# Stores of the scan's columns issued from GpSimd's queue instead of SyncE's, in a one-core RWKV-7 and neighbourhood-attention trunk

## Chip, cores and metric

The kernel runs on one core of a Trainium2 chip. The metric is the device time of one execution in microseconds, as a median of several executions. A core has five engines, each of which works through its own queue of instructions in order: TensorE (PE, with its weight loads PEld), VectorE (DVE), ScalarE (ACT), GpSimd (POOL) and SyncE (SP). In this kernel SP does nothing but issue DMA transfers. An instruction waits at the head of its engine's queue until the semaphores that it names are reached, and what stands behind it on that engine waits too.

## What is computed

Two independent requests (x_prompt and x_sample, 512 tokens of 1024 features each) go through two layers with shared weights. Layer 0 is a bidirectional RWKV-7 branch, layer 1 a gated neighbourhood attention. Cut to what matters:

```python
for i in range(2):                                   # layers
    xn = rms_norm(x, pre_norm_g[i])
    h = rwkv7(xn) if i == 0 else natten(xn)
    x = x + rms_norm(h, post_norm_g[i])

# rwkv7: r, k, v from token-shifted xn, z from xn (four 1024x1024 projections)
for d in range(2):                                   # forward and backward scan, 16 heads of 64
    S_t = S_(t-1) (diag(decay_t) + a_t b_t^T) + v_t k_t^T ;  y_t = S_t r_t
y = group_norm(y[0] + y[1]) + sum_d sum(r * k_d * r_k) * v
out = (y * silu(z)) @ w_o
# natten: q, k, v, z = split(xn @ w_in + b_in); windowed softmax attention; (o * silu(z)) @ w_ao + b_ao
```

## The kernel before

**Layout and tiles.** Activations lie with features on the 128 partitions and the 512 tokens of a request along the free axis, so that a tensor of a request is eight tiles of 128x512 f32 (256 KB). A request is called s = 0 or 1, and the eight tiles are p = 0 to 7 (a tile holds two heads). A projection is done a column at a time: one column is one output tile, 8 contraction tiles by 3 matmuls (lines 802 to 804 in the scan; weights and activations are each split in two parts, `whi` and `wlo`, `act` high and low). The weights of a column come in two loads `raw` of 128x512 through three buffers (NRAW), are split by ACT (line 721) and DVE (line 723), and wait in four buffers (NW).

**Stages.** A prelude normalises both requests, makes the z and k columns of request 0 and stores the shifted operands (`lk`, `lr`, `lv`, `lz`) of request 1 to DRAM. Then `scan_phase` (about 190 to 1180 us) does the scan: eight blocks (two requests by four pairs of tiles) of eight steps, 64 steps one after the other. Beside the steps, in the same phase, run: `flow` (the remaining columns, r and v of request 0, k, r, v and z of request 1, w_o of request 0, and 24 columns of layer 1), `prep` (per tile: decay, keys, the array `ab` that goes to DRAM as `dab`), `inverse` (DVE's elimination per block) and `finish` (per block: normalisation and gate, `dy`). Last, `rest` does the remaining projections, the attention and the output.

**What goes through DRAM.** `save(kind, s, p, src)` at line 323 makes a DRAM tile and stores `src` into it, from SP (line 325). Column results are written by ACT or DVE into `tmp` tiles (five buffers, NTMP) and saved as `dr`, `dk`, `dv`, `dz` and, for layer 1, `q1`, `k1`, `v1`, `z1` (named `dq`, `dk`, `dv`, `dz` in the profile). `prep` saves the head sums' products `ks` (line 968, `dks<-kp`). The v column is also transposed by TensorE (line 680), copied by ACT into `vs` (line 683, two buffers, NVS) and stored by token as `dvt`: four stores of 64x512 a column at lines 685 to 687, each of 512 runs of 256 bytes. The scan loads V (line 1047) and X (lines 1055 to 1057) from `dvt`, `prep` loads k and r, `finish` loads ks, v and z. All of these loads and stores stand in one queue, SP's.

**What POOL does.** In the scan phase only memsets: the border column of `e1` in `prep` (line 893, 32 of them) and half of `MT` in `inverse` (line 1014, 16).

**What sets the order.** PE, DVE and ACT follow in the scan phase an order written by a planner (`weave`, line 1600): threads for the parts above are taken by rank as soon as a model of the machine (`Clock`) says that their inputs are there. The model gives a DMA from SP 380 ns of its queue (line 131), a share of one common transfer queue (`dq`) and a landing time. Where the model sees PE without work it puts in a matmul whose result is not used (line 1626), to keep PE's clock up. The orders of SP's and POOL's queues are made by the scheduler of the tile framework, by the times at which it expects each instruction to be ready. A waiting instruction therefore holds up the ones that were placed behind it.

Of the kernel before, what the change touches and what calls it, by code (L numbers as in the profile page):

```python
# [19 lines left out]
P = 128  # L20
# [30 lines left out]
class Clock:  # L51
# [40 lines left out]
    def room(self, key, bufs):  # L92
        s = self.slots.get(key, ())
        return 0.0 if len(s) < bufs else min(self.left(n) for n in s)
# [18 lines left out]
    def one(self, e, i):  # L113
        ap = lambda xs: [x for x in xs if hasattr(x, "bass_ap")]
        outs, ins = ap(i.outs), ap(i.ins)
        if not outs:
            return 0.0
        name = lambda x: x.bass_ap.tensor.name
        t = issued = self.t[e]
        for table, xs in ((self.made, ins), (self.used, outs)):  # L120
            for x in xs:
                for f, at in table.get(name(x), {}).items():
                    if f != e or e == "S" or e in "AD" and table is self.made:
                        t = max(t, at)
        free = lambda x: int(np.prod([n for _, n in x.ap[1:]])) if len(x.ap) > 1 else 1
        n = max([free(outs[0])] + [free(x) for x in ins[:1]])
        if e == "P":
            t, done = self.matmul(i, ins, free(outs[0]), t)
        elif e == "S":

            self.t[e] = issued = max(issued, self.t["P"]) + 380.0
            size = outs[0].ap[0][1] * free(outs[0]) * 4
            c = size * 0.0027 + 150.0
            self.dq = max(issued + 800.0, self.dq) + c
            done = max(self.dq, t + 800.0 + c) + 670.0
        else:
            if e == "A":
                c = 85.0 + 0.85 * n
            elif e == "G":
                c = 150.0 + n  # L140
            else:
                kind = type(i).__name__
                sb = [x for x in ins if free(x) > 8 and not name(x).startswith(self.BANKS)]
                c = 82.0 + 1.02 * n
                if "Reciprocal" in kind:
                    c = 80.0 + 6.2 * n
                elif getattr(i, "is_tensor_tensor_scan", False):
                    c = 80.0 + 2.1 * n
                elif "Transpose" in kind:
                    c = 80.0 + 1.8 * n  # L150
                elif len(sb) == 1 and len(ins) <= 2 and "TensorTensor" not in kind and "Reduce" not in kind and free(outs[0]) == n:
                    c = 110.0 + 0.53 * n if not getattr(i, "is_scalar_tensor_tensor", False) else 130.0 + 1.06 * n
            self.t[e] = t + c
            done = t + c + self.LAT[e]
        for x in ins:
            u = self.used.setdefault(name(x), {})
            u[e] = max(u.get(e, 0.0), done)
            self.slot[name(x)] = True
        for x in outs:
            for table in (self.used, self.made):  # L160
                u = table.setdefault(name(x), {})
                u[e] = max(u.get(e, 0.0), done)
        return 0.0 if e == "S" and "dram" in str(type(outs[0].bass_ap.tensor)).lower() else done

    def matmul(self, i, ins, n, t):
        f32, tr = ins[0].dtype == F32, bool(i.is_transpose)
# [63 lines left out]
class Trunk:  # L230
# [17 lines left out]
    SUMS, SG, ZY = 0, 0, 2  # L248
# [22 lines left out]
    def name(self, s):  # L271
        self.uid += 1
        return f"{s}_{self.uid}"
# [29 lines left out]
    def t(self, tag, shape=(P, T), bufs=1, dt=F32, pool=None):  # L303
        x = (pool or self.main).tile(list(shape), dt, tag=tag, bufs=bufs, name=self.name(tag))
        self.clock.new(x.tensor.name, (tag, id(pool or self.main)), bufs)
        return x
# [15 lines left out]

    def save(self, kind, s, p, src):
        self.sp[kind, s, p] = d = self.dram(f"{kind}{s}{p}", src.shape)
        self.nc.sync.dma_start(d, src)

    def load(self, dst, src):
        self.nc.sync.dma_start(dst, src)
# [111 lines left out]
    def rstd(self, acc):  # L440
        run(self.rstds(acc))
        return acc
# [165 lines left out]
    def column(self, s, kind, p, ps):  # L608

        nc, sp = self.nc, self.sp  # L610
        vt, act = nc.vector, nc.scalar
        first = lambda e: (e, None, lambda c, n=ps.tensor.name: c.at([n]))
        keep, whole = self.clock.keep, ps.tensor.name
        if kind == "z":

            o, th = self.tmp(), self.tmp()
            if s == 0:
                yield first("D")
                vt.tensor_tensor(o, ps, self.rstd0, op=ALU.mult)
                ps = o  # L620
            yield "A" if s == 0 else first("A")
            keep.add(whole)
            act.activation(th, ps, AF.Tanh, scale=0.5)
            yield "D"
            keep.discard(whole)
            vt.scalar_tensor_tensor(o, th, 1.0, ps, op0=ALU.add, op1=ALU.mult)
            self.save("z", s, p, o)
            return
        yield "A", None, lambda c: max(c.at([ps.tensor.name]), min(c.room(("tmp", id(self.main)), self.NTMP), 1e10))
        o = self.tmp()  # L630
        if kind == "k":
            keep.add(whole)
        act.copy(o, ps)
        self.save(kind, s, p, o)
        if kind == "r":
            self.made.add((kind, s, p))
            return
        if kind == "k":
            yield "A"
            keep.discard(whole)  # L640
            sq = self.tmp()
            act.activation(sq, ps, AF.Square, scale=self.vec("kk", p))
            free, room = self.bank()
            yield "P", free, lambda c: max(room(c), c.at([sq.tensor.name]))
            ss = self.p("pm", (2, T))
            nc.tensor.matmul(ss, self.ssel, sq, start=True, stop=True)
            yield "A"
            row = self.tmp((2, T))
            act.copy(row, ss)
            if p == 0:  # L650
                sp["ss", s] = self.dram(f"ss{s}", (16, T))
            self.load(sp["ss", s][2 * p:2 * p + 2], row)
            self.made.add((kind, s, p))
            if p == NP - 1:
                yield "S", None, lambda c: c.at([sp["ss", s].tensor.name])

                rn = self.tmp((P, 64))
                self.load(rn, sp["ss", s].rearrange("a (b c) -> (a b) c", b=8))
                yield "A"
                act.activation(rn, rn, AF.Sqrt)  # L660
                yield "D"
                vt.tensor_scalar(rn, rn, 1e-12, None, op0=ALU.max)
                vt.reciprocal(rn, rn)
                sp["rn", s, 0] = self.dram(f"rn{s}", (16, T))
                self.load(sp["rn", s, 0].rearrange("a (b c) -> (a b) c", b=8), rn)
                self.made.add(("rn", s))
            return

        if p == 0:

            sp["vt", s] = self.dram(f"vt{s}", (4, 2, NCH // 2, 2, L, 2, 2, HD))
        yield "A"
        back = self.tmp()
        act.copy(back, o[:, ::-1])
        for d in range(2):
            free, room = self.bank()
            yield "P", free, lambda c: max(room(c), c.at([back.tensor.name]))
            vp = self.p("pm")
            for m in range(4):
                nc.tensor.transpose(vp[:, m * P:(m + 1) * P], (back if d else o)[:, m * P:(m + 1) * P], self.ident)  # L680
            yield "A", None, lambda c: max(c.at([vp.tensor.name]), c.room(("vs", id(self.main)), self.NVS))
            vs = self.t("vs", (P, 4, P), self.NVS)
            act.copy(vs, vp.rearrange("p (m c) -> p m c", m=4))
            for j in range(2):
                self.load(
                    sp["vt", s][p // 2, j, :, :, :, d, p % 2].rearrange("m h t c -> t (m h) c"),
                    vs[64 * j:64 * j + 64].rearrange("t m (h c) -> t (m h) c", h=2))
        self.made.add((kind, s, p))
# [952 lines left out]
    def scan_phase(self, mid):  # L1641
        t = lambda tag, shape: self.t(tag, shape, 1, F32, self.front)
        did = self.did
        self.mrx = t("mrx", (P, 2, 2, L))
        for d in range(2):
            self.nc.vector.tensor_copy(self.mrx[:, d], self.mr[d].unsqueeze(1).broadcast_to([P, 2, L]))
# [64 lines left out]
        e = mybir.EngineType  # L1711
# [4 lines left out]
    def run(self):  # L1716
# [2 lines left out]
        self.did = Counter()  # L1719
        self.xz, self.os = [], [[], []]  # L1720
        self.spare = None
        mid, prep, first = ExitStack(), ExitStack(), ExitStack()
        self.banks(mid, pf=1, pm=5 - self.SG - self.ZY, us=1)
        if self.SG:
# [18 lines left out]
        self.rest(prep, mid)  # L1743

    def rest(self, prep, mid):
        prep.close()
        mid.close()
        self.banks(self.stack, pg=self.PG, pt=self.PT, po=1, sc=1, pm=5 - self.PG - self.PT)
# [166 lines left out]
```

## Time and profile before

| | us |
|---|---|
| median of 3 runs | 1694.72 (1691.98 to 1698.94) |
| profiled execution, its own time | 1691.19 |
| span of the profiled execution | 1689.4 |
| prelude, 0 to 190: PE busy | 169.51 of 190 |
| scan phase, 190 to 1180: PE busy | 913.97 of 990 |
| rest, 1180 to 1690: PE busy | 488.80 of 510 |
| POOL busy in the whole span | 24.2 |
| mean granted TensorE clock | 0.971 |

The profile lists each engine's instructions with their times. Idle time in front of an instruction is put down to what released it. "SPq" rows are SP's DMA issues: their length is the time that SP's queue spent on issuing, not the transfer. A transfer's landing is seen only where an instruction waited for it. PE's records overlap, so a busy PE is not necessarily at its peak, and the matmuls of line 1626 count as busy although nothing uses them.

### The profile page before, as it was taken

To read this page: it belongs to the slowest core of one execution; us is meant where nothing else is said; L and a number is where in the kernel's file an instruction comes from. 1 tells how busy PE (TensorE), PEld (TensorE's weight loads), DVE (VectorE), ACT (ScalarE), POOL (GpSimd) and SP (SyncE) were. 2 spreads that over 40 slices of the span, in tenths; PEclk is the share of its full clock that TensorE was granted. 3 is DMA by queue.
4 is the path that set the end of the run, shared out by engine and by line. 5 is a ranking of instruction groups with operands and counts; after the bars stand their busy time and mean duration, and the time that the engine had idled before them with its cause. 6 is when DMAs were issued, how large, how long until landed. Compare 5 with 4: busy or idle time off the path is not lost. (4 is left out here: it accounts for less than half of the span.)

```text
span 1689.4 us, 46296 instructions
## 1 busy us (share of the span) xinstructions
PE 1572.3 (93%) x18820; PEld 1201.0 (71%) x18820; DVE 1229.1 (73%) x2725; ACT 982.1 (58%) x1977; POOL 24.2 (1%) x94
## 2 busy tenths in 40 slices
PE   7989888899988998989988999999999898999998
PEld 5767666676766766767766767777787687777776
DVE  8985668689678787887888888745676766465564
ACT  5443655677765768656566665444676655555562
POOL 0000000000000000000000000000000000000000
PEclk9989999899999999999998999999999899999999
DMA  5435678688587787775776765554765246545553
GB/s 208 162 125 187 202 231 260 181 253 267 183 262 229 215 263 238 229 245 181 231 254 209 220 206 165 171 186 138 269 205 172 86 124 240 189 149 176 167 176 106
DMA packets 240821, 336.26 MB, mean 199 GB/s; under 512 B 53696, under 2 KB 119360, under 8 KB 240608
## 3 DMA queue, kind: packets, MB, share of 16 engines
q1 hardware_dynamic: 240608, 333.31, 61.9%
q8 instruction: 148, 2.42, 0.6%
q14 instruction: 65, 0.53, 0.1%
HBM read 227.71 MB, written 105.51 MB: 197 GB/s over the span
## 5 line engine op out<-in xcount | busy, mean ns | idle before, releaser
L802 PE MATMUL pm<-act,whi 128*128 128x512 f32 x640 | 284.9, 445 | 17.2 <-ACT act L747 4.3
L804 PE MATMUL pm<-act,wlo 128*128 128x512 f32 x640 | 258.0, 403 | 10.0 <-DVE wlo L723 9.9
L803 PE MATMUL pm<-act,whi 128*128 128x512 f32 x640 | 258.4, 404 | 7.4 <-DVE act L749 6.4
L423 PE MATMUL pg<-act,whi 128*128 128x512 f32 x448 | 184.0, 412 | 3.1 <-ACT os L1494 1.9
L424 PE MATMUL pg<-act,whi 128*128 128x512 f32 x448 | 179.2, 400 | 4.8 <-DVE act L373 4.8
L425 PE MATMUL pg<-act,wlo 128*128 128x512 f32 x448 | 179.0, 399 | 0.0
L372 ACT CAST whi<-raw 128x512 fp32r<-128x512 f32 x148 | 91.3, 618 | 131.1 <-PE pg L424 87.2
L802 PEld LDWEIGHTS pm<-act,whi 128*128 128x128 f32 x640 | 122.8, 192 | 62.2 <-issue 11.5
L804 PEld LDWEIGHTS pm<-act,wlo 128*128 128x128 f32 x640 | 123.4, 193 | 42.2 <-DVE wlo L723 15.1
L803 PEld LDWEIGHTS pm<-act,whi 128*128 128x128 f32 x640 | 123.5, 193 | 33.3 <-DVE act L749 12.4
L373 DVE TENSOR_TENSOR wlo<-raw,whi 128x512 fp32r<-128x512 f32 x148 | 101.7, 689 | 61.7 <-ACT whi L372 56.2
L723 DVE TENSOR_TENSOR wlo<-raw,whi 128x512 fp32r<-128x512 f32 x160 | 109.1, 685 | 36.5 <-ACT whi L721 33.2
L721 ACT CAST whi<-raw 128x512 fp32r<-128x512 f32 x160 | 98.4, 617 | 58.1 <-PE pm L803 27.5
L424 PEld LDWEIGHTS pg<-act,whi 128*128 128x128 f32 x448 | 85.6, 191 | 22.0 <-DVE act L373 5.2
L423 PEld LDWEIGHTS pg<-act,whi 128*128 128x128 f32 x448 | 85.3, 191 | 21.9 <-issue 3.0
L425 PEld LDWEIGHTS pg<-act,wlo 128*128 128x128 f32 x448 | 85.5, 191 | 18.1 <-issue 0.7
L996 DVE TENSOR_TENSOR N<-etmp,N 128x30 f32<-128x30 f32 (+14 forms) x240 | 78.8, 328 | 4.2
L994 DVE TENSOR_TENSOR etmp<-N 128x30 f32<-128x30 f32 (+14 forms) x240 | 78.6, 328 | 4.1
L1448 DVE CUSTOM_DVE_ANT_0 sb<-sc,bias 128x256 f32<-128x256 f32 x128 | 49.9, 420 | 40.3 <-PE pt L1455 26.4
L1451 ACT ACTIVATE sb<-sb,mx 128x256 f32<-128x256 f32 x128 | 64.1, 503 | 11.0 <-DVE mx L1450 10.8
L1090 PE MATMUL pf<-cab 64*64 64x128 f32 (+1 forms) x2048 | 66.3, 265 | 1.9 <-issue 1.9
L1201 ACT COPY X<-us 64x256 f32<-64x256 f32 x128 | 47.0, 367 | 33.3 <-PE zy L1068 30.1
(389 smaller groups left out, 3370.9 us busy)
## 6 DMA issues: line engine op xcount, KB each, us to landing
dab<-ab SPq DMA_DIRECT2D x32, 1024.0 KB
cab<-dab SPq DMA_DIRECT2D x64, 512.0 KB
raw<-in_w_in_dram SPq DMA_DIRECT2D x128, 256.0 KB
bias<-in_rpb_dram SPq DMA_DIRECT2D x32, 384.0 KB
raw<-in_w_z_dram SPq DMA_DIRECT2D x32, 256.0 KB
dz<-tmp SPq DMA_DIRECT2D x32, 256.0 KB
raw<-in_w_k_dram SPq DMA_DIRECT2D x32, 256.0 KB
dk<-tmp SPq DMA_DIRECT2D x32, 256.0 KB
```

Of the source, the lines that this page charges most:

```text
L372: self.nc.scalar.copy(hi, src)
L373: (eng or self.nc.vector).tensor_tensor(lo, src, hi.bitcast(F32), op=ALU.subtract)
L423: nc.tensor.matmul(ps, hi, x[k][0], start=(k == 0), stop=False)
L424: nc.tensor.matmul(ps, hi, x[k][1], start=False, stop=False)
L425: nc.tensor.matmul(ps, lo, x[k][0], start=False, stop=(k == KT - 1))
L721: nc.scalar.copy(hi, raw[h])
L723: nc.vector.tensor_tensor(lo, raw.pop(h), hi.bitcast(F32), op=ALU.subtract)
L802: nc.tensor.matmul(ps, hi[:, at], xh, start=(k == 0), stop=False)
L803: nc.tensor.matmul(ps, hi[:, at], xl, start=False, stop=False)
L804: nc.tensor.matmul(ps, lo[:, at], xh, start=False, stop=(k == KT - 1))
L994: vt.tensor_tensor(tv, N[:, q + 1:, q:q + 1].broadcast_to([P, n, q]), N[:, q:q + 1, :q].broadcast_to([P, n, q]), op=ALU.mult)
L996: vt.tensor_tensor(N[:, q + 1:, :q], tv, N[:, q + 1:, :q], op=ALU.add)
```

## The change

While `scan_phase` runs (`self.away` is True there and False before and after), `save` issues its stores from POOL's queue for every kind except y, x1 and h, and so do the stores of v by token. These are 152 DMAs: 16 of r, 16 of v, 8 of k and 8 of z of layer 0, 16 of `ks`, 64 of `dvt`, and 6 each of q, k, v and z of layer 1. The small stores of k's sums of squares (`dss`), the stores of `ab`, y, x1 and h, and all loads stay on SP.

The planner's model is told of it: a DMA from POOL takes 900 ns of POOL's queue in the model, where one from SP takes 380, and its waits and landing are reckoned as an SP store's. Since the planner's times change, the whole order of PE, DVE and ACT in the scan phase is planned anew.

```diff
@@ Clock.one
-                    if f != e or e == "S" or e in "AD" and table is self.made:
+                    if f != e or e in "SG" or e in "AD" and table is self.made:
...
-        elif e == "S":
-
-            self.t[e] = issued = max(issued, self.t["P"]) + 380.0
+        elif e == "S" or type(i).__name__ == "InstDMACopy":
+            if e == "G":
+                self.t[e] = issued = max(issued, self.t["P"]) + 900.0
+            else:
+                self.t[e] = issued = max(issued, self.t["P"]) + 380.0
...
-        return 0.0 if e == "S" and "dram" in str(type(outs[0].bass_ap.tensor)).lower() else done
+        return 0.0 if e in "SG" and "dram" in str(type(outs[0].bass_ap.tensor)).lower() else done
@@ Trunk
     def save(self, kind, s, p, src):
         self.sp[kind, s, p] = d = self.dram(f"{kind}{s}{p}", src.shape)
-        self.nc.sync.dma_start(d, src)
+        self.store(kind).dma_start(d, src)
+
+    def store(self, kind):
+        return self.nc.gpsimd if self.away and kind not in ("y", "x1", "h") else self.nc.sync
@@ column
             for j in range(2):
-                self.load(
+                self.store("vt").dma_start(
                     sp["vt", s][p // 2, j, :, :, :, d, p % 2].rearrange("m h t c -> t (m h) c"),
@@ scan_phase
+        self.away = True
@@ run, rest
+        self.away = False
```

The instructions below are listed as they stand in each engine's queue, with the buffer numbers; line numbers of the changed kernel are 2 to 8 higher from line 130 on (line 802 is 807 there, 1626 is 1631).

POOL's queue in the scan's first part, before (`e1` is the array of decays of a prep, `MT0` the inverse's buffer of a block):

```order
L893 MEMSET e1_580_2300 128x8
L893 MEMSET e1_647_2551 128x8
L893 MEMSET e1_674_2686 128x8
L893 MEMSET e1_748_3091 128x8
L1014 MEMSET MT0_439_1696 32x32x32 x2
L893 MEMSET e1_779_3317 128x8
```

The same stretch of POOL's queue now (`tmp` is a column's result, `kp0` the product that is stored as `dks`, `vs` a transposed v tile):

```order
L898 MEMSET e1_666_2609 128x8
L327 DMA dks01_620_2457<-kp0_575_2246 128x512
L327 DMA dv00_645_2521<-tmp_644_2519 128x512
L327 DMA dv01_655_2575<-tmp_654_2573 128x512
L690 DMA dvt0_646_2523<-vs_670_2620 64x8x64 x2
L898 MEMSET e1_690_2752 128x8
L690 DMA dvt0_646_2523<-vs_672_2630 64x8x64 x2
L690 DMA dvt0_646_2523<-vs_684_2685 64x8x64 x2
L327 DMA dv02_695_2764<-tmp_694_2762 128x512
L898 MEMSET e1_765_3192 128x8
```

Between two memsets of `e1` there now stand up to eighteen stores, and a store can stand behind a memset: `dks01` and `dv00` come after the memset of e1_666.

SP's queue before, where the first v columns of request 0 are stored and the first step's V and X are loaded:

```order
L328 DMA raw_691_2790<-in_w_v_dram 128x512
L328 DMA dvt0_659_2585<-vs_695_2814 64x8x64 x2
L325 DMA dv02_700_2829<-tmp_699_2827 128x512
L325 DMA dks02_701_2832<-kp0_662_2597 128x512
L328 DMA dvt0_659_2585<-vs_702_2834 64x8x64 x2
L328 DMA X_705_2844<-dvt0_659_2585 64x2x128
L328 DMA raw_707_2851<-in_w_v_dram 128x512
L328 DMA tmp_713_2865<-in_lora2_dram 128x512
L328 DMA r_709_2858<-dr03_521_2015 128x512
L328 DMA raw_732_2988<-in_w_v_dram 128x512
L328 DMA dvt0_659_2585<-vs_718_2896 64x8x64
L328 DMA V_703_2838<-dvt0_659_2585 128x256
```

The same place of SP's queue now:

```order
L333 DMA dab01_632_2489<-ab_668_2615 128x8x256
L333 DMA raw_700_2783<-in_w_v_dram 128x512
L333 DMA rb_733_2997<-drn0_411_1636 64x512 x2
L333 DMA X_699_2780<-dvt0_646_2523 64x2x128
L333 DMA X_727_2950<-dvt0_646_2523 64x2x128
L333 DMA raw_721_2933<-in_w_v_dram 128x512
L333 DMA k_731_2995<-dk03_302_1318 128x512
L333 DMA dab01_632_2489<-ab_692_2758 128x8x256
L333 DMA V_697_2774<-dvt0_646_2523 128x256
L333 DMA X_699_2780<-dvt0_646_2523 64x2x128
L333 DMA V_698_2777<-dvt0_646_2523 128x256
```

The stores `dvt`, `dv` and `dks` are gone from between the loads, and the loads of V and X wait here for stores that another queue issues.

PE's queue after the first r column, before (line 1626 is the matmul without use, 872 and 873 the decays of the first prep, 802 to 804 a product of the next column):

```order
L1626 MATMUL zy_444_1710<-cc_143 128x256 x2
L872 MATMUL pm_480_1835<-h0_126_633,w2h_472_1793 128x512
L873 MATMUL pm_480_1835<-h0_126_633,w2l_471_1792 128x512
L1626 MATMUL zy_444_1710<-cc_143 128x256
L872 MATMUL pm_486_1848<-h2_137_669,w2h_472_1793 128x512
L873 MATMUL pm_486_1848<-h2_137_669,w2l_471_1792 128x512
L1626 MATMUL zy_444_1710<-cc_143 128x256
L802 MATMUL pm_487_1853<-act_414_1641,whi_482_1840 128x512
L803 MATMUL pm_487_1853<-act_413_1640,whi_482_1840 128x512
```

And now:

```order
L1631 MATMUL zy_444_1710<-cc_143 128x256 x3
L877 MATMUL pm_480_1836<-h0_126_633,w2h_472_1793 128x512
L878 MATMUL pm_480_1836<-h0_126_633,w2l_471_1792 128x512
L1631 MATMUL zy_444_1710<-cc_143 128x256
L877 MATMUL pm_486_1849<-h2_137_669,w2h_472_1793 128x512
L878 MATMUL pm_486_1849<-h2_137_669,w2l_471_1792 128x512
L807 MATMUL pm_487_1853<-act_414_1641,whi_482_1841 128x512
L808 MATMUL pm_487_1853<-act_413_1640,whi_482_1841 128x512
```

From here on the two orders differ everywhere. Over the whole program PE's queue holds 98 matmuls of line 1626 before and 105 now; 108 products (threes of lines 802 to 804) stand ahead of the first scan step's outputs (line 1213) before and 129 now, with 44 and 35 matmuls of line 1626; behind the first output of the last step there are 27 products before and 16 now, and none and 3 matmuls of line 1626.

More of the change, by code (lines that the diff above doesn't have):

```diff
@@ L1745, in rest @@
     def rest(self, prep, mid):
+        self.away = False
         prep.close()
```

## The prediction

> **What bounds the kernel now.** I read the head of the page first, then the busy time of each stage, then who waits for whom in the scan phase on PE, ACT and SP, then the rows of the stores that move. The change acts between 190 and 1180 us alone; a row of stages shows what room is there.
>
> ```profile
> span 1689.4 us, 46296 instructions
> PE 1572.3 (93%) x18820; PEld 1201.0 (71%) x18820; DVE 1229.1 (73%) x2725; ACT 982.1 (58%) x1977; POOL 24.2 (1%) x94
> ...
> 190.00:1180.00 990.00, 913.97 (x15391) 688.52 (x15391) 767.75 (x1481) 609.22 (x1184) 18.70 (x47) 0.97 0.69 217
> ...
> L1626 PE MATMUL zy<-cc 128*128 128x256 f32 x196 | 50.0, 391 | 0.5 <-ACT Z L1174 0.5
> ```
>
> In the scan phase PE is busy 914 of 990 us, so 76 us are idle; 47 to 50 us of the busy time are the matmuls that nothing uses. PE's other work does not change. So the phase can become shorter by part of some 125 us at most, and it becomes longer by whatever stalls PE anew. DVE, with 768 of 990, is the second engine. Next, what PE's idle time was waiting for:
>
> ```profile
> PE pm L804 <- DVE wlo L723: 9.9, 9, 3.5
> PE pm L803 <- DVE act L749: 6.4, 11, 2.4
> ...
> PE pm L802 <- ACT act L747: 4.3, 5, 1.9
> ...
> PE zy L1068 <- DMA cab<-dab: 2.7, 2, 1.5
> ```
>
> ```profile
> ACT whi L721 <- DMA raw<-in_w_r_dram: 9.6, 3, 4.8
> ACT whi L721 <- DMA raw<-in_w_v_dram: 9.5, 4, 4.7
> ```
>
> PE waited directly for a load for 2.7 us only. Late weights reach it through ACT's and DVE's splits (lines 721, 723, 747 and 749); these waits are 9.9 + 6.4 + 4.3 us, and ACT waited for r's and v's weights 9.6 and 9.5 us. So 9.9 + 6.4 + 4.3 + 2.7 = 23.3 us is all of PE's idle time in these rows that earlier loads could remove, if each of them were a load's fault.
>
> **What leaves SP.** The rows of the issues (least, median and longest in ns) price it, and a piece of SP's order in time shows the place where it is densest:
>
> ```profile
> L325 SPq DMA_DIRECT2D dz<-tmp x32: 319/326/732, 44.5 to 1645.2; - x32
> L325 SPq DMA_DIRECT2D dk<-tmp x32: 319/359/1548, 99.5 to 1611.7; - x32
> L325 SPq DMA_DIRECT2D dv<-tmp x32: 319/422/1493, 266.0 to 1620.3; - x32
> ...
> L325 SPq DMA_DIRECT2D dr<-tmp x16: 319/330/1638, 185.4 to 551.2; - x16
> L325 SPq DMA_DIRECT2D dks<-kp x16: 319/392/622, 214.0 to 1000.3; - x16
> ...
> L325 SPq DMA_DIRECT2D dq<-tmp x16: 319/377/435, 942.1 to 1603.4; - x16
> ...
> L328 SPq DMA_DIRECT2D dvt<-vs x64: 574/626/1738, 274.8 to 685.4; - x64
> ```
>
> ```profile
> 274.85 2.77 SPq L328 DMA_DIRECT2D dvt<-vs x4
> ...
> 281.96 2.22 SPq L328 DMA_DIRECT2D dvt<-vs x2
> ...
> 390.85 1.56 SPq L328 DMA_DIRECT2D dvt<-vs x2
> ```
>
> Of the moved stores 14 are dz, 14 dk, 22 dv, 16 dr, 16 dks, 6 dq and 64 dvt. At the medians: 14 x 0.326 + 14 x 0.359 + 22 x 0.422 + 16 x 0.330 + 16 x 0.392 + 6 x 0.377 + 64 x 0.626 = 73 us of SP's 990. That is SP's time, and SP is not the bound, as its longest waits show:
>
> ```profile
> SPq L328 <- DVE wlo L723: 116.8, 74, 8.6
> SPq L328 <- PE zy L1213: 77.8, 44, 4.0
> ...
> SPq L325 <- ACT tmp L633: 30.3, 17, 6.0
> ```
>
> SP stands 117 us before loads of weights because their buffer is still being split, and 78 us before loads of X because the step is still using it. Both remain. What goes is that loads stand behind a store whose data are not there yet (30 us after ACT's copy of a column). The relief reaches PE only where a load was late, so it lies between 0 and -23.3 us. I take -2: the direct row is 2.7, and the other three rows name DVE and ACT, which are short of time themselves (DVE 768 of 990).
>
> **What POOL gets.** No DMA of POOL stands in the trace. What does is its memsets and how long they wait:
>
> ```profile
> L1014 POOL MEMSET MT<- 32x1024 f32 x16 | 15.1, 947 | 243.2 <-ACT MT L1013 242.6
> L893 POOL MEMSET e<- 128x8 f32 x32 | 3.7, 115 | 641.7 <-DVE ab L916 567.5 <-ACT sq L1263 35.0 <-ACT whi L721 23.9
> ...
> POOL e L893 <- DVE ab L916: 567.5, 28, 46.6
> ```
>
> POOL is free, but its queue is full of waits: a memset of `e1` stands until DVE has read the array before it, up to 46.6 us. A store placed behind such a memset waits with it, and a memset placed behind a store waits for the column's copy; ahead of DVE's read of `e1` there are usually many us, so the second costs nothing while the queue runs roughly as ordered. Queued behind a late store are the next memsets and stores; who waits for these are SP's loads of k, r, ks, v, V and X (and every load behind them on SP), ACT where it wants a `vs` or `tmp` back, and DVE for `e1`.
>
> The price of one issue on POOL is bounded below by SP's 0.32 us for 128 rows. Above, the nearest row with 512 runs is SP's own longest dvt issue, 1.74 us. I take 0.9, which the change's model assumes and which lies between. Over SP's typical 0.38 that is 0.52 more; a v column has four `dvt` stores in a row, so its last lands 4 x 0.52 = 2.1 us later, with nothing else in the way. In eight blocks these stores gate the first V and X: at most 8 x 2.1 = 17 us, at least 0. Block 0 and the first block of request 1 follow their v columns closely, the others have theirs well ahead. So two to three of eight count: 2.5 x 2.1 = 5 us. The Trainium skill (DMA: Bandwidth & Descriptors, Specifications) gives about 1 us to the first byte for a DMA from GpSimd and 0.6 for one from SP; by that, 0.4 more a store, 8 x 4 x 0.4 = 13 us would be the most. It is an estimate from the page, and no run shows it yet.
>
> **The new order.** The planner's model moves the PE order. 196 records of line 1626 are 98 matmuls in the order (each is recorded twice): 50.0 / 98 = 0.51 us each. With 105 it is 7 x 0.51 = +3.6 us that the plan fills with nothing useful, a sign that it expects PE to be short of work for longer. The end of the scan shifts as well:
>
> ```profile
> 268.09 0.39 PE L802 MATMUL pm<-act,whi 128*128 128x512 f32 x1
> 268.32 0.40 PE L803 MATMUL pm<-act,whi 128*128 128x512 f32 x1
> 268.56 0.40 PE L804 MATMUL pm<-act,wlo 128*128 128x512 f32 x1
> 268.79 0.39 PE L872 MATMUL pm<-h,w2h 128*128 128x512 f32 x1
> ```
>
> ```profile
> 1156.16 0.64 PE zy L1213 x16
> 1156.83 0.44 DVE y L1230
> ...
> 1177.55 0.44 PE pm L1288 x4
> ```
>
> A product takes 268.79 - 268.09 = 0.70 us. Behind the last step's outputs there were 27 products, 18.9 us, about as long as the chain of the last `finish` from 1156.8 to 1177.6; with 16 they are 11.2. The 7.7 us of cover that are lost can be taken by the columns of `rest`, whose inputs are ready, where a bank of PSUM is free. So 0 to 7.7; I take 2. If the cover were gone altogether, the finish chain would cost its 20.7 less 11.2.
>
> **Sum.** -2 + 5 + 3.6 + 2 = +8.6 us. The profiled execution took 1691.19 us, 1.8 more than its span and 3.5 less than the median; the same added to the median gives 1694.72 + 8.6 = 1703.3, rounded 1703. With all terms at their ends the forecast's own range is 1694.7 - 23.3 + 3.6 = 1675 and 1694.7 + 17 + 3.6 + 7.7 = 1723; that all ends come together I hold for unlikely, so its own eight in ten are 1694 to 1715.
>
> **Rivals.**
>
> *Faster, since SP's queue was the hidden cause (0.27).* Each load is issued earlier, weights stay ahead of the splits, and the plan's reserve is not needed. For it speak the dense dvt issues from 274.85 and the 9.5 us that ACT waited for v's weights; against it that the long SP waits are for buffers. Half of the 23.3 us would be 11.7: 1694.7 - 11.7 = 1683, and with the plan's 3.6 on top 1687.
>
> *POOL's queue becomes the bound in the v columns (0.13).* The 32 dvt stores of a request lie between 274.85 and about 393 us, 118 us. At 0.9 they use 29 of these. It decides from 118 / 32 = 3.7 us a store: then `vs`, with two buffers, is not free, ACT waits at line 683 with everything behind it on ACT, and PE gets no split weights. At 5 us a store, as a mixture of issue and of waiting behind memsets, the excess is 32 x 5 - 118 = 42 us in request 0, and if the second request hides it, 1694.7 + 42 = 1737. Against it stands that the longest issue of a dvt on SP was 1.74. The Trainium skill (SBUF — State Buffer, § SBUF: two separate sides) has a rule by which this would happen at much smaller loads: GpSimd cannot write descriptors while DVE holds the shared port in a two-port operation, and it reports 620 ns becoming about 3100. At 3.1 us, 32 stores would need 99 of the 118 us, still under the point. The page also says that tensor_tensor has no two-port form. That is what most of DVE's work in this phase is, for one:
>
> ```profile
> L994 DVE TENSOR_TENSOR etmp<-N 128x30 f32<-128x30 f32 (+14 forms) x240 | 78.6, 328 | 4.1
> ```
>
> *No change to speak of (0.25).* The stores were off the path and still are, and the new order is as good as the old: 1694.7, give or take 6. For it speaks that PE's waits name a DMA for 2.7 us only.
>
> **How the numbers follow.** The forecast, a modest loss, has 0.35, the others as given. About 0.5%, 8.5 us, is what a measurement of this kernel can tell from no change. The forecast's case lies just on that bound; I give 0.30 of its 0.35 to slower (late landings tend to add up along queues that run in order), and 0.05 to the same. The rival without change lies within the bound, POOL's is beyond it, and of the rival that is faster nearly all is. So faster 0.27, same 0.30, slower 0.43. The range from 1682 to 1728 leaves out the far end of POOL's case and the part of the faster case beyond half of the 23.3 us.
>
> **What would show it.** Right: PE's busy time in the scan phase grows by the 7 matmuls; the rows of waits name POOL for ACT or DVE in few places only; dvt issues on POOL near 1 us; SP's waits gain rows for dvt, dk or dr of some us. Relief: ACT's waits for raw in r and v fall well below 19 us. Wrong, to the slow side: ACT waiting at line 683 for dvt, DVE for `e1`, a granted clock under 0.97. Wrong, to the fast side: PE idle in the scan phase well under 76 us and fewer waits of DVE's splits.

## The result, and the profile after

| | before | after |
|---|---|---|
| median, us | 1693.35 (1687.33 to 1698.94, 4 runs) | 1675.66 (1673.62 to 1678.02, 4 runs) |
| ratio to before | | 0.990 (95% interval 0.9873 to 0.9928) |
| profiled execution, span | 1689.4 | 1671.8 |
| scan phase, 190 to 1180: PE busy | 913.97 | 923.48 |
| POOL busy in the whole span | 24.2 | 116.9 |
| mean granted TensorE clock | 0.971 | 0.974 |

The change gained 1.0%, 17.7 us, where a loss of 8.6 us was forecast; 1675.66 lies under the range's lower end of 1682. The head of the page after, span and busy time of each engine:

```profile
span 1671.8 us, 46461 instructions
...
PE 1566.5 (94%) x18834; PEld 1200.3 (72%) x18834; DVE 1229.4 (74%) x2725; ACT 982.8 (59%) x1977; POOL 116.9 (7%) x246
```

DVE and ACT do what they did (1229.1 and 982.1 before). PE's work differs by the 14 records of the matmuls without use. The span became 17.6 us shorter with the same work: PE's idle time fell by 11.8 us (117.1 to 105.3), and its busy time by 5.8, at a mean granted clock of 0.974 instead of 0.971. The scan phase in the view by stages (length, then busy time of PE, PEld, DVE, ACT, POOL, clock, DMA share, GB/s):

```profile
190.00:1180.00 990.00, 923.48 (x15450) 698.92 (x15450) 772.79 (x1489) 614.14 (x1191) 110.29 (x197) 0.97 0.69 219
```

PE is idle 66.5 us there instead of 76.0. The groups of the matmuls without use and of three kinds of moved stores (busy us, mean ns of one, then the idle time before them):

```profile
L1631 PE MATMUL zy<-cc 128*128 128x256 f32 x210 | 55.0, 396 | 0.5 <-ACT y L1233 0.5
...
L690 POOL DMA_DIRECT2D dvt<-vs x64 | 44.7, 703 | 87.4 <-ACT vs L688 85.4 <-issue 2.0
...
L327 POOL DMA_DIRECT2D dv<-tmp x22 | 12.2, 557 | 128.4 <-ACT tmp L638 77.9 <-ACT tmp L1406 50.5
...
L327 POOL DMA_DIRECT2D dks<-kp x16 | 8.8, 548 | 81.6 <-DVE kp L972 73.8 <-DVE etmp L999 7.8
```

POOL issues a `dvt` in 0.70 us and a store of 128 rows in 0.55; its queue stands idle before them, waiting for the data. Who waits for whom, over the whole execution (us in total, times, longest):

```profile
POOL e L898 <- DVE ab L921: 165.4, 23, 23.4
...
PE zy L1173 <- DMA V<-dvt: 6.4, 1, 6.4
...
ACT whi L726 <- DMA raw<-in_w_r_dram: 4.8, 3, 2.2
ACT whi L726 <- DMA raw<-in_w_v_dram: 4.6, 1, 4.6
```

Two rows answer to the prediction's. ACT's waits for the weights of r and v fell from 9.6 + 9.5 to 9.4 us, as if SP had been relieved. And PE waits 6.4 us for V, once, which it did not do before. SP's own waits for buffers did not shrink (116.8 and 77.8 us before):

```profile
SPq L333 <- DVE wlo L728: 154.0, 79, 13.5
SPq L333 <- PE zy L1218: 106.7, 53, 8.4
```

So the profile after shows a gain that looks like SP's relief, and a loss that looks like POOL's queue. Which of the two parts of the change makes which, the queue or the order that is planned anew, it cannot tell.

### The profile page after: what moved, and what is told of

It reads as the page before. It is cut to its first block, busy times and chain, and to the rows that moved or that the text cites. A ratio compares the mean times of both kernels' runs of the same rounds, so it can differ in the third digit from the quotient of the medians.

```text
span 1671.8 us, 46461 instructions
## 1 busy us (share of the span) xinstructions
PE 1566.5 (94%) x18834; PEld 1200.3 (72%) x18834; DVE 1229.4 (74%) x2725; ACT 982.8 (59%) x1977; POOL 116.9 (7%) x246
## 4 chain that ended last, share of the span: by engine, by line
PE 68%; DVE 12%; DMA 9%; ACT 7%; issue 4%; SPq 1%; DVEq 0%; ACTq 0%
PE pm L807 7%; PE pm L808 5%; PE pm L809 5%; PE pg L428 5%; PE pg L429 5%; PE pg L430 5%; PE pf L1095 3%; PE zy L1167 2%; PE us L1214 2%; PE sc L1442 2%; PE us L1194 2%; PE zy L1218 2%; PE po L1475 2%; PE pt L1460 2%; DMA dab<-ab 1%
## 5 line engine op out<-in xcount | busy, mean ns | idle before, releaser
L807 PE MATMUL pm<-act,whi 128*128 128x512 f32 x640 | 285.5, 446 | 12.7 <-ACT act L776 4.1
L429 PEld LDWEIGHTS pg<-act,whi 128*128 128x128 f32 x448 | 84.9, 190 | 17.2 <-issue 1.7
```

What stands on the lines that cost most here:

```text
L429: nc.tensor.matmul(ps, hi, x[k][1], start=False, stop=False)
L807: nc.tensor.matmul(ps, hi[:, at], xh, start=(k == 0), stop=False)
```

## The experiments

### The two parts apart

`plan_only`: the planner reckons as in the change, but every store still goes out from SP. (`aside` holds the names of what the 152 stores write.) PE, DVE and ACT then hold the changed kernel's order, row for row.

```diff
+        if e == "S" and name(outs[0]) in self.aside:
+            e = "G"
@@ save, column
-        self.store(kind).dma_start(d, src)
+        self.nc.sync.dma_start(d, src)
```

> The order of PE, DVE and ACT is the changed kernel's, instruction by instruction, but all 152 stores are issued from SP. Theory A (SP's queue was in the way; the move itself pays): about 1693, ratio 0.995 to 1.005, since SP is as full as before. Theory B (the planner, told of another price, happened to write a better order): about 1676, ratio 0.99. A mixture: between.

Measured: 1664.81 us, ratio 0.9835 (0.979 to 0.9879).

`queue_only`: POOL issues the 152 stores, the planner reckons them as SP's. The order of the scan phase is that of before; a few instructions of the last part differ.

```diff
+        if e == "G" and type(i).__name__ == "InstDMACopy":
+            e = "S"
```

> The 152 stores go out from POOL, but the planner reckons them as SP's, so that the order of PE, DVE and ACT in the scan phase is the one of before. Theory A: about 1676, ratio 0.99. Theory B: about 1693, ratio 0.995 to 1.005. If the two are worth something only together (loads that start earlier need an order that uses them), both single parts stay near 1.00.

Measured: 1691.39 us, ratio 0.9997 (0.9973 to 1.002).

The whole gain and more is in the order; the move between queues gains nothing on the order of before, and takes 0.65% (0.9835 to 0.990, some 11 us) from the new one, though there the two intervals just touch. The waits of ACT for weights between 190 and 1190 us show that the relief was not the queue's. In plan_only, with all stores on SP:

```profile
ACT whi L732 <- DMA raw<-in_w_r_dram: 4.2, 2, 2.2
ACT whi L732 <- DMA raw<-in_w_v_dram: 3.7, 1, 3.7
```

In queue_only, with the stores on POOL:

```profile
PE zy L1175 <- DMA V<-dvt: 1.9, 1, 1.9
...
ACT whi L728 <- DMA raw<-in_w_r_dram: 9.6, 3, 4.8
...
ACT whi L728 <- DMA raw<-in_w_v_dram: 5.0, 3, 3.0
```

The new order has the shorter waits without any help from POOL (7.9 us). Moving the stores alone shortens v's from 9.5 to 5.0 us, and r's not at all, and the time stands still.

### Half of the stores each

`cols_pool` issues 88 stores (columns and `ks`) from POOL and the 64 `dvt` from SP; `dvt_pool` the other way round. Both have the changed kernel's order of PE, DVE and ACT in the scan phase.

```diff
@@ cols_pool, against plan_only: save
-        self.nc.sync.dma_start(d, src)
+        self.store(kind).dma_start(d, src)
@@ dvt_pool, against plan_only: column
-                self.nc.sync.dma_start(
+                self.nc.gpsimd.dma_start(
```

> The order of PE, DVE and ACT is the changed kernel's in the scan phase; the 88 stores of columns and head sums go out from POOL, the 64 of dvt from SP. On this order all stores from SP gave 0.9835, all from POOL 0.990. If POOL's cost lies in dvt (V and X are waited for by the scan's steps): near 0.9835, and no wait of PE for V. If it lies in each moved store: about 0.988 (88 of 152).

> The same order; only the 64 stores of dvt go out from POOL, the rest from SP. If POOL's cost lies in dvt: near 0.990, with a wait of PE for V of some us before the first step and a first step some 6 us later than with all stores on SP. If it lies in each moved store: about 0.986.

Measured: cols_pool 1669.35 us, 0.9873 (0.983 to 0.9916); dvt_pool 1668.16 us, 0.9869 (0.9834 to 0.9904). By the ratios both lie between plan_only and the change, about 6 us above the one and 5 below the other, and the intervals overlap: the times don't tell which group of stores costs. The wait of PE for V, which was expected of dvt_pool, isn't in its trace.

### Other prices in the planner, and so other orders

If the order makes the gain, is it a better order for a reason, or another draw? Only the number of nanoseconds was changed in these: in s370, s379, s381, s390 and s400 the 380 of before (all stores reckoned and issued on SP), in p600, p850, p899 and p1000 the 900 of plan_only (stores reckoned as POOL's, issued by SP), in g600 and a899 the 900 of the change itself (issued by POOL).

```diff
@@ s379
-            self.t[e] = issued = max(issued, self.t["P"]) + 380.0
+            self.t[e] = issued = max(issued, self.t["P"]) + 379.0
@@ p899, a899
-                self.t[e] = issued = max(issued, self.t["P"]) + 900.0
+                self.t[e] = issued = max(issued, self.t["P"]) + 899.0
```

> The changed kernel with 600 ns instead of 900 in the planner for a DMA of POOL; the changed kernel's rows show 540 ns for a store of 128 rows and 703 for one of dvt. Theory A: as the changed kernel, 0.99 with a few tenths of a per cent of scatter. Theory B: an order drawn anew, anywhere from 0.985 to 1.005.

> The kernel before with 400 ns instead of 380 in the planner for a DMA of SP, nothing else: a new order with no change of queue. It measures how far the time moves when only the order is drawn anew. Theory A: within 0.5% of before. Theory B: moves by up to 1% either way.

> The kernel before with 381 ns instead of 380 in the planner: a change of the model by a thousandth of a microsecond a DMA, which still writes another order. If the time of an order is a matter of chance within 1 to 1.5%: any ratio from 0.98 to 1.015, not 1.000. If only a real change of the model moves it: 0.998 to 1.002.

> The same with 379 ns. By chance: another ratio than that of 381, anywhere from 0.98 to 1.015. Otherwise 0.998 to 1.002.

> A further order, drawn with 899 instead of 900 ns for a store of POOL, all stores issued by SP. If orders scatter by chance with before an unlucky one, it lies anywhere from 0.98 to 1.01, likelier under 1 than over. If it is the reckoning with a cheap SP and dear stores that makes a good order, it lies within 0.3% of 0.9835.

> The order of the kernel with 600 ns a store of POOL (1.0148 with POOL issuing), all stores issued by SP. If the order alone makes that loss: 1.008 to 1.015, with PE's idle time at 890 to 990 us as before (17 us). If the loss was POOL's issue after all: within 0.5% of 1.000 or below.

> All stores issued by SP, the plan reckons a store of POOL with 1000 ns. Theory D, reckoning these stores as dear and off SP's queue makes the planner's orders better: 0.980 to 0.988, like 900 and 899. Theory E, any change of the price draws another order with a scatter of some 1%: anywhere from 0.98 to 1.01, with no tie to 900's.

> The same with 850 ns. Theory D: 0.980 to 0.990. Theory E: anywhere from 0.98 to 1.01.

> The plan of before with 370 instead of 380 ns a DMA of SP, all stores reckoned and issued on SP. Theory D: with nothing reckoned on POOL the orders stay behind, 0.989 to 1.003. Theory E: anywhere from 0.98 to 1.01.

> The same with 390 ns. Theory D: 0.989 to 1.003. Theory E: anywhere from 0.98 to 1.01, and below 0.988 would speak against D.

Measured, with every store issued by SP, so that the order alone differs (and in it the number of matmuls without use, 87 to 136):

| reckoned as | price, ns | median, us | ratio to before |
|---|---|---|---|
| SP's | 370 | 1688.76 | 0.9989 (0.9973 to 1.0006) |
| SP's | 379 | 1673.22 | 0.9895 (0.9858 to 0.9933) |
| SP's (before) | 380 | 1691.23 to 1693.35 | 1 |
| SP's | 381 | 1677.71 | 0.9928 (0.9901 to 0.9954) |
| SP's | 390 | 1679.51 | 0.9935 (0.9913 to 0.9957) |
| SP's | 400 | 1672.71 | 0.9896 (0.9862 to 0.9929) |
| POOL's | 600 | 1702.39 | 1.0064 (1.004 to 1.0089) |
| POOL's | 850 | 1685.65 | 0.9958 (0.9941 to 0.9974) |
| POOL's | 899 | 1667.03 | 0.9857 (0.9827 to 0.9886) |
| POOL's (plan_only) | 900 | 1664.81 | 0.9835 (0.979 to 0.9879) |
| POOL's | 1000 | 1705.53 | 1.0086 (1.0071 to 1.0102) |

899 and 900 wrote the same order, as their traces show: in those of p899 and plan_only the rows of DVE and ACT and SP's issues agree one for one, and PE's but for four neighbours that swap places. So these are ten orders, one of them timed twice (0.9835 and 0.9857). That pair also says what a second measurement of the same kernel can differ by, 0.2%.

The two groups overlap: 0.9895 to 1 where the stores are reckoned as SP's, 0.9835 to 1.0086 where as POOL's, and means of 0.994 and 0.999. Both ends belong to POOL's. One nanosecond in the planner, which changes nothing on the chip but the order, takes 0.7 to 1.05% off before. That the reckoning of dear stores makes better orders was one of the expectations; 600 and 1000 ns are slower than before, and it falls. The price only draws another order. Ten orders scatter by 0.8% about a mean of 0.996, seven of the nine others are at or below the order of before, and the change's is the best of all. They aren't independent of each other: by the rows of DVE and ACT, s381 keeps the order of before up to 899 us, s390 up to 673 and s400 up to 485.

What an order does badly can be read for one of the slow ones. The stage in which layer 1's columns begin, in p600:

```profile
890.00:990.00 100.00, 82.81 (x1132) 63.04 (x1125) 82.74 (x158) 54.37 (x104) 0.23 (x2) 0.90 0.73 234
```

and in plan_only:

```profile
890.00:990.00 100.00, 96.31 (x1785) 73.60 (x1786) 84.37 (x170) 66.94 (x131) 0.47 (x4) 0.95 0.59 196
```

PE is idle 17.2 of 100 us in the one and 3.7 in the other, with its clock at 0.90 against 0.95. The loss of before against plan_only is not in one such place. The starts of every eighth of the 64 scan steps (first scan output, us):

| | 1 | 9 | 17 | 25 | 33 | 41 | 49 | 57 | 64 | last product |
|---|---|---|---|---|---|---|---|---|---|---|
| before | 329.5 | 443.7 | 564.6 | 671.5 | 785.1 | 915.1 | 1040.8 | 1110.8 | 1156.1 | 1181.3 |
| plan_only | 332.0 | 433.6 | 541.8 | 658.2 | 774.6 | 908.5 | 1019.0 | 1094.1 | 1140.2 | 1158.0 |
| after | 337.9 | 441.4 | 550.6 | 668.5 | 786.4 | 919.7 | 1030.1 | 1105.1 | 1151.3 | 1169.1 |
| p600 | 325.4 | 432.6 | 537.2 | 649.5 | 755.9 | 871.2 | 1017.2 | 1082.2 | 1127.3 | 1189.9 |

Block by block plan_only gains and loses against before: 12.6 us in the first block, 12.7 in the second, then it gives back 9.5 in the third, and gains 15.2 again in the sixth (915.1 to 1040.8 against 908.5 to 1019.0). p600 has the fastest scan of the four and the latest last product: it ran the steps ahead at the cost of the columns. The sums from 190 us to the last product, in before:

```profile
190.00:1181.30 991.30, 915.27 (x15397) 689.58 (x15397) 768.28 (x1481) 609.22 (x1184) 18.70 (x47) 0.97 0.69 217
```

and in plan_only:

```profile
190.00:1158.00 968.00, 905.82 (x15404) 686.07 (x15403) 766.37 (x1479) 608.52 (x1184) 18.74 (x47) 0.98 0.69 221
```

PE's idle time falls from 76.0 to 62.2 us, and its busy time by 9.4 us although it has the seven further matmuls without use to do, with the granted clock at 0.98 instead of 0.97: together the 23.3 us by which the last product comes earlier. Why one order waits less than another is told by no single row; that stays open.

### The queue on four orders

The same orders with the stores issued by POOL: queue_only on that of before, q379 on that of s379, a899 on that of p899, g600 on that of p600, and the change on that of plan_only. The rows of 899 and 900 are one order, measured twice.

> The plan drawn with 379 instead of 380 ns a DMA of SP (0.9895 of before with all stores on SP), and now the 152 stores issued by POOL on that same order. Theory A, the queue is a cost of its own whatever the order (11 us on the order of after): 1673 + 11 = 1684, ratio 0.993 to 0.999. Theory B, the queue costs only where an order lets loads follow stores closely, as the order of after does at its first step: within 0.3% of 0.9895. Theory C, the queue pays: below 0.985.

> The change itself with 899 instead of 900 ns, so the order of the kernel ahead of it in this call (p899), with the 152 stores issued by POOL. Theory A: 0.65% above p899 (between 0.4 and 0.9%). Theory B: between 0 and 0.9% above, and where it is above, PE waits for V or X loaded from dvt. Theory C: below p899 by 0.3% or more. And if the gain of the change is a matter of the draw, its ratio to before need not be 0.990; over 1.000 would show that one nanosecond takes the whole gain back.

| order | stores by SP | stores by POOL | more | PE waits for V at the first step, us |
|---|---|---|---|---|
| 380, before | 1 | 0.9997 (0.9973 to 1.002) | 0.0% | 1.9 |
| 379 | 0.9895 | 0.9911 (0.9875 to 0.9946) | 0.2% | 7.2 |
| 899 | 0.9857 | 0.9895 (0.9863 to 0.9927) | 0.4% | 6.5 |
| 900, the change | 0.9835 | 0.990 (0.9873 to 0.9928) | 0.65% | 6.4 |
| 600 | 1.0064 | 1.0148 (1.0098 to 1.0198) | 0.8% | 5.2 |

On no order did POOL's queue pay. On single pairs the intervals overlap or nearly so; that all five pairs go from nothing to the slow side is what speaks. g600 came out slower than either theory had allowed, since its order alone costs 0.64% (p600) where 0.8 to 1.5% was expected, and the queue the rest. With SP issuing, PE's wait for V isn't there in any of these orders (it is in s370 with 2.7 us and in p850 with 2.3, which were not run from POOL). Where it comes from stands in SP's queue of the change, in time (start, us, line, transfer):

```profile
279.26 0.38 SPq L333 DMA_DIRECT2D dab<-ab  x1
279.74 1.88 SPq L333 DMA_DIRECT2D V<-dvt  x1
281.67 2.07 SPq L333 DMA_DIRECT2D X<-dvt  x1
283.84 1.59 SPq L333 DMA_DIRECT2D V<-dvt  x1
```

and in that of plan_only:

```profile
278.93 0.81 SPq L338 DMA_DIRECT2D V<-dvt  x2
279.78 0.60 SPq L338 DMA_DIRECT2D X<-dvt  x1
280.48 0.54 SPq L338 DMA_DIRECT2D dab<-ab  x1
```

`dab` is a store of 1024 KB; the next load from `dab` goes out at 287.84. With `dvt` on POOL the scheduler put V behind it; that it expected V's data later is likely, but not shown. PE's first use of V, in the change:

```profile
287.88 0.71 PE L1173 MATMUL zy<-V,AK 64*64 64x64 f32 x16 [6.38 <-DMA V<-dvt]
```

and in plan_only:

```profile
281.95 0.46 PE L1179 MATMUL zy<-V,AK 64*64 64x64 f32 x16 [2.25 <-DVE AK L1124]
```

V arrives 8.1 us after its issue in the one (279.74 to 287.88), in at most 3.0 in the other (278.93 to 281.95, where PE waited for DVE). The clock goes with it. The 20 us behind that point in the change:

```profile
280.00:300.00 20.00, 13.62 (x106) 11.12 (x106) 14.57 (x35) 4.49 (x9) 3.64 (x6) 0.74 0.79 242
```

and in plan_only:

```profile
280.00:300.00 20.00, 18.05 (x150) 14.87 (x151) 16.58 (x34) 8.65 (x15) 1.90 (x2) 0.91 0.95 280
```

The other kernels bear it out. In a899 and q379 dab stands ahead of both V as well, by 0.6 and 1.2 us; in p899, s379, cols_pool and dvt_pool it stands behind the first V, and PE doesn't wait for V. In g600 dab is long gone, and it is `cab`, a load of 512 KB, behind which V goes out, 3.3 us later than in p600 (290.54 and 287.21). In before and queue_only both V are issued more than 11 us after dab, which fits that the move cost nothing there.

dvt_pool separates the place in the queue from POOL itself. All 64 `dvt`, those that this V reads among them, go out from POOL, and SP's queue is:

```profile
278.66 0.78 SPq L338 DMA_DIRECT2D V<-dvt  x1
279.49 0.73 SPq L338 DMA_DIRECT2D X<-dvt  x1
280.31 0.63 SPq L338 DMA_DIRECT2D dab<-ab  x1
```

PE's first use of V there has the same wait for DVE as in plan_only:

```profile
282.89 0.46 PE L1179 MATMUL zy<-V,AK 64*64 64x64 f32 x16 [2.25 <-DVE AK L1124]
```

### Four stores back

That V stands behind dab can be undone with few stores. `tile1_sp` is the change with four of its 152 stores back on SP: the `dvt` of tile 1 of request 0. `again` is the change once more, on the same chip.

```diff
@@ column (the planner reckons all of them as POOL's)
-                self.store("vt").dma_start(
+                (self.nc.sync if s == 0 and p == 1 else self.nc.gpsimd).dma_start(
```

> The change once more, unchanged, as the companion of the next run: 0.990 of before within its interval (0.987 to 0.993), with PE's wait of 6.4 us for V at the first scan step, and the 1024 KB store dab issued ahead of that V on SP.

> The change with only four of its 152 stores put back on SP: the dvt of tile 1 of request 0, on which the first step's V waits. PE, DVE and ACT keep their order through the scan; on SP both V of the first two steps now stand ahead of dab. Theory F, the queue's cost at the first step is V behind a 1 MB store: PE's wait for V (6.4 us) is gone, PE waits some 2 us for DVE there as with all stores on SP, the first scan output comes 4 to 6 us earlier, and the time is 3 to 6 us below the companion. Rival G, V is late because POOL issues its stores late or slowly, or because DMAs of two queues get in each other's way, whatever stands ahead on SP: the wait stays above 4 us and the time within 2 us of the companion.

Measured: again 1674.53 us, 0.9893 (0.987 to 0.9915), with the wait of 6.5 us for V; tile1_sp 1667.40 us, 0.9851 (0.9828 to 0.9874). SP's queue in tile1_sp:

```profile
280.56 0.33 SPq L338 DMA_DIRECT2D V<-dvt  x1
280.94 0.60 SPq L338 DMA_DIRECT2D X<-dvt  x1
281.64 0.53 SPq L338 DMA_DIRECT2D V<-dvt  x1
282.27 0.38 SPq L338 DMA_DIRECT2D dab<-ab  x1
```

and PE's longest wait from 255 to 300 us:

```profile
PE zy L1179 <- DVE AK L1124: 2.2, 1, 2.2
```

The wait is gone, and with it 7.1 of some 10 us by which the change is slower than plan_only, though 148 stores are still POOL's (the intervals of again and tile1_sp still touch). The four stores that went back are ones that V reads, so this run alone would also fit late stores of POOL's; with dvt_pool, where they stay on POOL and V doesn't wait, that rival falls. One part doesn't fit: the gain of the medians is more than the 3 to 6 us expected, while in the profiled executions the first scan output comes only 2.6 us earlier (332.2 against 334.8) where 4 to 6 were expected, and the spans differ by 2.5 us (1663.9 and 1666.4). Against plan_only, product by product, tile1_sp is 1.5 us late at the 107th (298 us) where again is 5.1 late. At the 329th (689 us) they are 5.3 and 6.9 late, and from the 500th on (974 us) both some 5. So a second loss lies between 620 and 690 us, where the last columns' stores of request 1 go out. The 25 us from 640 on, in plan_only and then in tile1_sp:

```profile
640.00:665.00 25.00, 20.98 (x537) 15.98 (x536) 17.46 (x30) 19.82 (x42) 0.12 (x1) 0.93 0.85 250
640.00:665.00 25.00, 23.09 (x497) 17.52 (x489) 14.29 (x21) 19.15 (x39) 6.28 (x11) 0.66 0.74 223
```

The granted clock is 0.66 there against 0.93. On this order it is 0.66 to 0.73 in all five traces with `dvt` on POOL (the change, again, a899, tile1_sp, dvt_pool), and 0.93 in all three with `dvt` on SP (plan_only, p899, cols_pool). So this loss goes with the `dvt` stores' queue and a lower clock; what lowers the clock wasn't tried and stays open.

## Why the prediction was wrong

**The step that failed is "The new order".** It read the 7 further matmuls without use as a plan that expects PE to be short of work, and priced them at +3.6, with +2 for the end of the scan. They are there: 50.0 us became 55.0. But they don't price an order: plan_only, s390 and s370 all have 105 in their orders and stand at 0.9835, 0.9935 and 0.9989. Only the two with far more, p600 (136) and p1000 (121), are the two slowest. The end of the scan didn't cost either: from the last product to the end of the span it is 1689.4 - 1181.3 = 508.1 us before and 1671.8 - 1169.1 = 502.7 after. In place of +5.6 the order brought -1.65%, some -28 us (-1.4% where the same order was timed again), and nothing that the prediction read in it told of this: it is a draw from a scatter that the prediction had no term for. That the change came out faster at all is the luck of that draw.

**The relief of SP, -2,** can't be measured apart from POOL's cost: the queue alone, both together, gave 0.9997 on the order of before, where -2 + 5 = +3 us had been added. The rival that made it the cause of a gain came nearest to the time, with 1683, by a mechanism that isn't the one: ACT's waits for weights fell to 7.9 us with the order alone, and the queue alone, which took 4.5 us off v's, left the time where it was.

**POOL's queue, +5,** was right in kind. PE waits for the first V, and the queue costs from nothing to 0.8%, 11 us on the change's order. Its working was not: the issue costs 0.70 us where 0.9 was taken, and the 0.38 that was subtracted is not SP's price of a `dvt`, which the prediction's own row gives as 0.63; so four in a row lose 0.3 us and not 2.1. What costs is that V is placed behind a large store, at one place rather than in two to three blocks of eight, the idle time with the lowered clock behind it, and the second loss from 620 to 690 us, whose cause is open.

**POOL as the bound** fell. The point from which it decides was 3.7 us a store. The groups give 0.703, and the rows of the issues (least, median, longest in ns):

```profile
L690 POOL DMA_DIRECT2D dvt<-vs x64: 697/697/724, 264.5 to 688.3; - x64
```

The Trainium skill (SBUF — State Buffer, § SBUF: two separate sides) has a lock by which such a DMA took about 3100 ns beside a DVE copy. The 64 issues, with DVE busy for 773 of 990 us, show none of it; that agrees with the Trainium skill's remark there that tensor_tensor has no two-port form.

**No change to speak of** was the better forecast for the queue alone, and wrong for the kernel.

## What to carry to other kernels

Where a change also redraws a planned order, run the plan without the change and the change without the plan: here the first was worth -1.65% and the second nothing, and the result of both together didn't tell the two apart. Before a per cent is put down to an idea, move a price of the planner by a little, look whether the order really changed (899 and 900 ns wrote the same one), and see what that does; and if orders scatter by 0.8%, time ten of them, keep the best and time it again (plan_only, 1664.81 us, beats both kernels, and did so again as p899, 1667.03). A load that an engine waits for should not stand in a queue behind a large store that is needed later, and a change of queue for one transfer can move that order for others.

## What was not expected of the hardware

Stored from POOL, `dvt` makes far fewer packets. The page's lines on DMA in dvt_pool, where these 64 stores alone are POOL's:

```profile
DMA packets 210102, 336.27 MB, mean 202 GB/s; under 512 B 20928, under 2 KB 86592, under 8 KB 209888
...
q0 software_dynamic: 3072, 8.39, 2.3%
```

and in plan_only, where SP issues them:

```profile
DMA packets 240822, 336.26 MB, mean 203 GB/s; under 512 B 53697, under 2 KB 119361, under 8 KB 240609
```

The packets under 512 B fall by 32,769, which is 64 x 512 but for one; in their place are 3072, of 8.39 MB / 3072 = 2.7 KB. It gained no time here (0.9869 against 0.9835).

A load behind a large transfer of its queue is late by microseconds. In q379, where V stands behind dab, the view of the transfers from 275 to 300 us has a landing (KB, us from the issue; an issue's landing is seen only where something waited for it):

```profile
V<-dvt SPq DMA_DIRECT2D x3, 128.0 KB, 7.1
```

The Trainium skill (DMA: Bandwidth & Descriptors, Queues, rings and completion order) says that descriptors of one queue are consumed in ring order on each DMA engine; the traces agree: 7.1 us in this row and 8.1 in the change, the latter counted from the start of the issue, behind 1024 KB, against at most 3.0 ahead of it.

And the clock fell to half within some 4 us of PE's standing still, as the stages of 2 us in the change show:

```profile
282.00:284.00 2.00, 0.00 (x0) 0.00 (x0) 2.00 (x5) 0.17 (x1) 1.39 (x2) 0.90 1.00 307
284.00:286.00 2.00, 0.00 (x0) 0.00 (x0) 1.87 (x5) 0.00 (x0) 0.57 (x1) 0.50 1.03 257
```

PE's last matmuls ahead of the wait began at 280.45; from 284 to 286 the granted clock is 0.50, and the first matmuls of 128x512 after the wait took 0.63 us each where they took 0.40 before it.
